# The junction of output projection and MLP: first products begun earlier, odd tiles in PSUM, four squares added later

## The chip, the cores and the metric

One core of one Trainium2 chip runs the kernel; the other cores take no part. The metric is the device time of one execution in microseconds. The program is written with a planner: the kernel's text gives the order of work and its dependencies, the planner lays out each engine's queue from its own costs and then sets the semaphores. Each engine works through its queue in order. Only where the text pins TensorE's instructions do they keep the order of the text.

## The reference, cut to what matters

Two layers; layer 0 mixes with gated DeltaNet, layer 1 with sliding-window attention. Both end in an output projection, and the same gated MLP follows:

```python
for i in range(DEPTH):                       # 2 layers
    hn = rmsnorm(h, norm_mix[i])
    mix = deltanet_mixer(hn, ...) if i % 2 == 0 else swa_mixer(hn, ...)   # ... @ w_out
    h = h + mix
    h = h + conv_ffn(rmsnorm(h, norm_ffn[i]), f_w_up[i], f_conv[i], f_w_down[i])
    gate = sigmoid(rmsnorm(h, norm_ple[i]) @ ple_w_gate[i])
    h = h + gate * (p[i] @ ple_w_proj[i])
return rmsnorm(h, norm_final)

def conv_ffn(x, w_up, conv_w, w_down):
    u = causal_dwconv(x @ w_up, conv_w)      # 1024 -> 2 * 2816, three taps
    gate, val = u[..., :D_FF], u[..., D_FF:]
    return (silu(gate) * val) @ w_down
```

Sequence and model width are 1024, all data f32.

## The kernel before, in words

Activations lie transposed: a tile is 128 channels (partitions) by 1024 positions, two halves of 512; `hs(h)` is a half. h has eight tiles, m = 0 to 7. TensorE multiplies f32 by splitting each operand into a high part (a cast to fp32r, on ScalarE) and a low part (the rest, by a subtraction) and adding three products, high x high, high x low, low x high, in one PSUM bank (`mm3`, L152). For weights the subtraction is on POOL (`load_w`, L199; `halves`, L1193), for activations on VectorE or POOL.

The output projection has two parts. Its first takes the first five mixer tiles (`NP1`) and is fed to TensorE between the mixer's own instructions (`first`). Its last part, `finish`, takes the other three: for each m it loads weights of 384 columns (`add`, with `load_w`), makes 2 x 9 products, and adds the two halves to h (the evictions, L848). Then `Mix.add` prepares the MLP's input from that tile. It stores h in DRAM (hf, L903), scales it by the norm's weight (L906, xw), and forms what the MLP's matrix scheme wants from each pair of an even and an odd tile. The MLP's up projection takes a 2 x 2 block product with seven half-size products in place of eight: of the even tile's halves it needs b11 and t1 (L913, L910), of even and odd tile t2, t3, t4 (L919, L922, L923), of the odd tile b21 and b22, each split in high and low part (`pair`, L897 and L898). At the end the tile is squared and added to the norm's sum (L261, L262).

The MLP, `ffn`, runs over 22 steps j of gate and value tile. Its weights come from two raw tiles a step (L1183, three raw buffers), combined by VectorE into s1 (L1211), s2 (L1212, L1219) and s3 (L1214), and cast and subtracted half by half into three buffers (L1192, L1193); `take` keeps four ahead. A step makes the products b11, t2, t3, t1, b21, t4, b22 with VectorE and ScalarE combining them in PSUM and z1, z2; rows of the norm's factor (`rb`) scale them, and the causal conv (`taps`, L309) and the gate follow, one step later (`gated`). In j = 0 the first four products go k by k, and the sum of squares is closed (`nrm.factor`: 16 small products) right behind them. From j = 2 on, steps of the down projection (`step`, L1285 to L1298) run between: each loads 256 raw columns (`draw`, three buffers) and a tile of h, adds two halves and stores it.

PSUM has three banks for `mm`, three for `d`, two for `s` (`pst`). SBUF working tiles are 40 slots, each given out again after its last use.

TensorE's order is pinned in both mixers and in the MLP; `finish` runs with the pin off.

Of the kernel before, what the change touches and what calls it, by code (L numbers as in the profile page):

```python
# [16 lines left out]
P = 128  # L17
# [91 lines left out]
def kernel(  # L109
# [202 lines left out]
    def delta_layer():  # L312
# [513 lines left out]
        E.pinned = False  # L826
        return op.finish(2, 0)

    class OutProj:
# [13 lines left out]

        def add(self, m, xs, k0):
            t = self.h[m]
            ps2 = proj(self.w[m, :, k0 * P:(k0 + len(xs)) * P], xs)
            for h in range(2):
                V.tensor_tensor(t[:, hs(h)], t[:, hs(h)], ps2[h], ADD)  # L848
# [17 lines left out]
        def finish(self, nxt, l):  # L866
            xs = self.parts(NP1, KT)
            mix = Mix(nxt, l)
            for m in range(KT):
                self.add(m, xs, NP1)  # L870
                if m == KT - 1:
                    for a, b in xs:
                        S.put(a, b)
                mix.add(m, self.h[m])
            return mix

    class Mix:
# [5 lines left out]
        def __init__(self, nxt, l):  # L883
# [3 lines left out]
            self.slots = {n: [] for n in self.x}  # L887

# [3 lines left out]
        def pair(self, t, name, names, eng):  # L892

            hi = S.get(name + "h", F32R)
            lo = S.get(name + "l", F32R)
            for h in range(2):
                A.copy(hi[:, hs(h)], t[:, hs(h)])  # L897
                eng.tensor_tensor(lo[:, hs(h)], t[:, hs(h)], hi[:, hs(h)].bitcast(F32), SUB)  # L898
                self.x[names[h]].append((hi[:, hs(h)], lo[:, hs(h)]))
            self.slots[names[-1]] += [hi, lo]  # L900

        def add(self, m, t):
            nc.sync.dma_start(self.hf[m], t[:, 0:T])  # L903
            xw = S.get("xw")
            for h in range(2):
                A.activation(xw[:, hs(h)], t[:, hs(h)], AF.Copy, scale=self.nrm.w[:, m:m + 1])  # L906
            a, b = hs(0), hs(1)
            if m % 2 == 0:
                self.t12 = S.get("t12")
                V.tensor_tensor(self.t12[:, a], xw[:, a], xw[:, b], SUB)  # L910
                bb = S.get("b11", F32R)
                A.copy(bb[:, a], xw[:, a])
                V.tensor_tensor(bb[:, b], xw[:, a], bb[:, a].bitcast(F32), SUB)  # L913
                self.x["b11"].append((bb[:, a], bb[:, b]))
                self.slots["b11"].append(bb)
                self.xw = xw
            else:
                t12, x0 = self.t12, self.xw
                V.tensor_tensor(t12[:, b], xw[:, b], t12[:, a], ADD)  # L919
                self.pair(t12, "t12", ("t1", "t2"), V)  # L920
                t34 = S.get("t34")
                V.tensor_tensor(t34[:, a], x0[:, b], xw[:, b], SUB)  # L922
                V.tensor_tensor(t34[:, b], xw[:, a], t12[:, b], SUB)  # L923
                S.put(t12, x0)
                self.pair(t34, "t34", ("t3", "t4"), G)
                S.put(t34)
                self.pair(xw, "x1", ("b21", "b22"), G)
                S.put(xw)
            self.nrm.square(t)
            S.put(t)  # L930


    def swa_layer(xs, nrm, hd):
# [235 lines left out]
        E.pinned = False  # L1169
        return op.finish(3, 1)  # L1170
# [4 lines left out]
    def ffn(l, mix, nxt):  # L1175
        nrm, hf = mix.nrm, mix.hf
        E.pinned = True
# [98 lines left out]
        def load_step():  # L1276
# [3 lines left out]
            w = wp.tile([P, 2 * P], F32, tag="draw", name="draw", bufs=3)  # L1280
            nc.sync.dma_start(w, f_down[l, m, :, a * P:(a + 2) * P])
            hi = wp.tile([P, 2 * P], F32R, tag="dhi", name="dhi", bufs=2)
            lo = wp.tile([P, 2 * P], F32R, tag="dlo", name="dlo", bufs=2)
            t = S.get("h")
            nc.sync.dma_start(t[:, 0:T], hf[m])  # L1285
            A.copy(hi, w)  # L1286
            G.tensor_tensor(lo, w, hi[:, :].bitcast(F32), SUB)  # L1287
# [15 lines left out]
        def up(j, early, late):  # L1303
# [6 lines left out]
            if j == 0:  # L1310
                w = take(4)
                ps = [pmt(), pdt(), pmt(), pmt()]
                for k in range(KT // 2):
                    for p, v, xn in zip(ps, w, ("b11", "t2", "t3", "t1")):
                        prod(p, v, xn, (k,))
                p1, p6, p7, p5 = ps
# [4 lines left out]
                nrm.factor()  # L1321
            else:
# [7 lines left out]
                V.tensor_tensor(dd, p6, dd, SUB)  # L1330
                for _ in range(early[1]):
# [12 lines left out]
            if j == 0:  # L1344
                prod(p7, *take(), "t4", first=False)
                rb.extend(nrm.banks())
                A.copy(zh(z1, 0), p1)
                V.tensor_tensor(zh(z1, 0), zh(z1, 0), rb[0], MUL)
                V.tensor_tensor(zh(z2, 1), zh(z2, 1), rb[1], MUL)
            else:  # L1350
                A.copy(zh(z1, 0), p1)
                V.tensor_tensor(zh(z1, 0), zh(z1, 0), rb[0], MUL)
                prod(p7, *take(), "t4", first=False)
            done("t4")
            V.tensor_tensor(zh(z2, 0), p7, dd, ADD)
            V.tensor_tensor(zh(z2, 0), zh(z2, 0), rb[0], MUL)
            for _ in range(late[0]):
                step()
            ys[j] = taps(2 * j + 1, z2)
# [3 lines left out]
            V.tensor_tensor(zh(z1, 1), zh(z1, 1), rb[1], MUL)  # L1363
# [3 lines left out]
        def down(j0, xs):  # L1367
# [31 lines left out]
            return fx, nn  # L1399

# [146 lines left out]
    hT, fx, nrm, ps_in = ffn(0, delta_layer(), 4)  # L1547
# [82 lines left out]
```

## Time and profile before

| | us |
|---|---|
| median of 3 runs | 2816.38 (2813.0 to 2822.61) |
| the profiled execution | 2815.47 |
| its span, first to last instruction | 2813.8 |
| TensorE busy | 2669.6 |
| VectorE busy | 1799.4 |
| ScalarE busy | 1108.4 |
| POOL busy | 1177.4 |

The profile names engines PE (TensorE), DVE (VectorE), ACT (ScalarE), POOL and SP (the queue that issues DMAs). A group of instructions stands as line, engine, operation, written tile <- read tiles and shape. An entry such as "[1.88 <-DVE h L1297]" says how long the engine was idle ahead of an instruction, and what ended that. Times run from the span's start. Busy times of neighbours on VectorE and ScalarE overlap by some 0.08 us, so a queue without a gap shows starts closer together than durations.

### The profile page before, as it was taken

Reading aid. Unit: us, or ns where it says so; the run is one execution under the profiler, and the core shown is the slowest. Engines: PE = TensorE matmul, PEld = TensorE weight load, DVE = VectorE, ACT = ScalarE, POOL = GpSimd, SP = SyncE. Lnnn points to the kernel's source line nnn. Section 1 sums busy time; section 2 is a strip of 40 time slices with the busy share of each in tenths; the row PEclk is TensorE's granted clock in tenths of the full one; section 3 lists DMA queues with packets and bytes.
Section 4 is the critical chain, followed back from the end, with each engine's and each line's share of the span. In section 5 each row is a group of like instructions: output and inputs, shape, how many; then the busy total and the mean of one; then the engine's idle time right before and its main releaser. Section 6 shows DMA issues by size and latency. Waiting matters only on the chain. (4 is left out here: it accounts for less than half of the span.)

```text
span 2813.8 us, 35193 instructions
## 1 busy us (share of the span) xinstructions
PE 2669.6 (95%) x12914; PEld 2144.8 (76%) x12914; DVE 1799.4 (64%) x2491; ACT 1108.4 (39%) x2134; POOL 1177.4 (42%) x1038
## 2 busy tenths in 40 slices
PE   9999999999699999999999998998899999999997
PEld 7777877778487887877777776676677888888786
DVE  6555555563877677677764346646677776767755
ACT  5433433342533333333343235644333333333443
POOL 5444343331654444444432322224544444444344
PEclk9999999999899999999999999999899999999998
DMA  4322222122225555555432221212255555564323
GB/s 171 87 70 63 71 56 63 48 93 61 98 97 182 182 176 199 196 183 178 154 107 77 86 57 45 64 57 95 72 169 184 182 184 186 182 205 159 110 90 107
DMA packets 167070, 340.83 MB, mean 121 GB/s; under 512 B 38897, under 2 KB 91505, under 8 KB 166897
## 3 DMA queue, kind: packets, MB, share of 16 engines
q1 hardware_dynamic: 166032, 337.20, 36.4%
q8 instruction: 101, 1.65, 0.2%
q10 hardware_dynamic: 864, 1.38, 0.1%
q14 instruction: 73, 0.59, 0.1%
HBM read 232.56 MB, written 99.68 MB: 118 GB/s over the span
## 5 line engine op out<-in xcount | busy, mean ns | idle before, releaser
L199 POOL TENSOR_TENSOR wlo<-wraw,whi 128x1024 fp32r<-128x1024 f32 (+4 forms) x138 | 260.6, 1891 | 455.3 <-ACT whi L198 421.0
L152 PE MATMUL mm<-xh,whi 128*128 128x512 f32 x856 | 357.7, 418 | 1.1 <-DVE gt L304 1.0
L152 PE MATMUL mm<-xh,wlo 128*128 128x512 f32 x856 | 349.7, 409 | 0.9 <-POOL wlo L199 0.8
L152 PE MATMUL mm<-xl,whi 128*128 128x512 f32 x856 | 346.4, 405 | 2.5 <-DVE xl L243 2.5
L1287 POOL TENSOR_TENSOR dlo<-draw,dhi 128x256 fp32r<-128x256 f32 x144 | 142.6, 990 | 309.1 <-ACT dhi L1286 287.4
L1193 POOL TENSOR_TENSOR wlo<-sa,whi 128x512 fp32r<-128x512 f32 x132 | 197.5, 1497 | 169.7 <-ACT whi L1192 169.6
L1193 POOL TENSOR_TENSOR wlo<-wraw,whi 128x512 fp32r<-128x512 f32 x132 | 194.6, 1481 | 138.8 <-ACT whi L1192 138.8
L152 PE MATMUL d<-gh,dhi 128*128 128x512 f32 x576 | 229.7, 399 | 12.1 <-DVE h L1297 12.1
L152 PE MATMUL d<-gh,dlo 128*128 128x512 f32 x576 | 227.8, 396 | 0.0
L152 PE MATMUL d<-gl,dhi 128*128 128x512 f32 x576 | 227.8, 395 | 0.0
L1297 DVE TENSOR_TENSOR h<-h,d 128x512 f32<-128x512 f32 x288 | 193.8, 682 | 32.2 <-PE d L152 31.4
L198 ACT CAST whi<-wraw 128x1024 fp32r<-128x1024 f32 (+4 forms) x138 | 108.2, 786 | 266.8 <-PE mm L152 110.5
L152 PEld LDWEIGHTS mm<-xh,wlo 128*128 128x128 f32 x856 | 163.2, 191 | 35.6 <-POOL wlo L199 1.7
L152 PEld LDWEIGHTS mm<-xl,whi 128*128 128x128 f32 x856 | 163.8, 191 | 29.3 <-DVE xl L243 3.4
L152 PEld LDWEIGHTS mm<-xh,whi 128*128 128x128 f32 x856 | 163.6, 191 | 27.9 <-issue 2.0
L309 DVE SCALAR_TENSOR_TENSOR yf<-zg,fcv,yf 128x1024 f32<-128x1024 f32 x88 | 134.9, 1533 | 21.4 <-ACT yf L307 19.9
L152 PEld LDWEIGHTS d<-gh,dhi 128*128 128x128 f32 x576 | 108.2, 188 | 44.9 <-DVE h L1297 15.6
L152 PE MATMUL mm<-t34h,whi 128*128 128x512 f32 x352 | 140.4, 399 | 0.0
L152 PE MATMUL mm<-t34l,whi 128*128 128x512 f32 x352 | 140.4, 399 | 0.0
L152 PE MATMUL mm<-t34h,wlo 128*128 128x512 f32 x352 | 140.2, 398 | 0.0
L152 PE MATMUL mm<-x1h,whi 128*128 128x512 f32 x352 | 139.5, 396 | 0.0
L152 PE MATMUL mm<-x1h,wlo 128*128 128x512 f32 x352 | 139.2, 396 | 0.0
(370 smaller groups left out, 6611.7 us busy)
## 6 DMA issues: line engine op xcount, KB each, us to landing
hf<-h SPq DMA_DIRECT2D x160, 512.0 KB, 3.4
h<-hf SPq DMA_DIRECT2D x160, 512.0 KB, 4.2
wraw<-f_up SPq DMA_DIRECT2D x88, 512.0 KB, 3.4
draw<-f_down SPq DMA_DIRECT2D x144, 128.0 KB, 2.3
wraw<-a_in SPq DMA_DIRECT2D x32, 512.0 KB, 3.4
wraw<-g_w SPq DMA_DIRECT2D x24, 512.0 KB, 3.3
row<-rowd SPq DMA_DIRECT2D x16, 512.0 KB, 3.8
wraw<-b_in SPq DMA_DIRECT2D x12, 512.0 KB, 3.6
```

Source lines behind the costliest of these rows:

```text
L152: i = nc.tensor.matmul(*a, **k)
L198: A.copy(hi, raw)
L199: G.tensor_tensor(lo, raw, hi[:, :].bitcast(F32), SUB)
L309: V.scalar_tensor_tensor(dst[:, 0:T], z[:, i:i + T], w[:, i:i + 1], dst[:, 0:T], MUL, ADD)
L1193: G.tensor_tensor(lo, src, hi.bitcast(F32), SUB)
L1287: G.tensor_tensor(lo, w, hi[:, :].bitcast(F32), SUB)
L1297: V.tensor_tensor(t[:, hs(h)], t[:, hs(h)], ps, ADD)
```

## The change

The MLP becomes a generator that `finish` starts: it takes its first four weights ahead of the last part, makes the k = 0 products of b11 and t1 behind tile 5, and the rest of the first four products behind tile 7. The last part's weights get small buffers of their own (`load_small`, two deep, shared with the down steps, whose raw buffers go from three to two). In `Mix.add` the odd tile is scaled into two PSUM banks (`pst`), and the low parts of b21 and b22 go from POOL to VectorE. Tiles 4 to 7 are squared in place, and their adds and the closing of the sum come later in j = 0. The scaling of j = 0's outputs by the norm's factor and its first conv go to j = 1. TensorE stays pinned from the mixer through the MLP.

```diff
+    def load_small(src, n):
+        raw = wp.tile([P, n], F32, tag="draw", name="draw", bufs=2)
+        nc.sync.dma_start(raw, src)
+        hi = wp.tile([P, n], F32R, tag="dhi", name="dhi", bufs=2)
+        lo = wp.tile([P, n], F32R, tag="dlo", name="dlo", bufs=2)
+        A.copy(hi, raw)
+        G.tensor_tensor(lo, raw, hi[:, :].bitcast(F32), SUB)
+        return hi, lo
...
-        def finish(self, nxt, l):
+        def finish(self, nxt, l, nple):
+            mix = Mix(nxt, l)
+            mlp = ffn(l, mix, nple)
+            next(mlp)
             xs = self.parts(NP1, KT)
-            mix = Mix(nxt, l)
+            E.pinned = True
             for m in range(KT):
-                self.add(m, xs, NP1)
+                t = self.h[m]
+                wh, wl = load_small(self.w[m, :, NP1 * P:], (KT - NP1) * P)
+                for h in range(2):
+                    ps = pdt()
+                    mm3(ps, wh, wl, xs, h)
+                    V.tensor_tensor(t[:, hs(h)], t[:, hs(h)], ps, ADD)
...
+                mix.add(m, t)
+                if m == 5:
+                    next(mlp)
+            return mlp
...
+        def part(self, n, src, hi, lo, eng):
+            A.copy(hi, src)
+            eng.tensor_tensor(lo, src, hi.bitcast(F32), SUB)
+            self.x[n].append((hi, lo))
...
             if m % 2 == 0:
+                x0 = S.get("x0")
+                for h in (a, b):
+                    A.activation(x0[:, h], t[:, h], AF.Copy, scale=w)
                 bb = S.get("b11", F32R)
+                self.part("b11", x0[:, a], bb[:, a], bb[:, b], V)
+                t12 = S.get("t12")
+                V.tensor_tensor(t12[:, a], x0[:, a], x0[:, b], SUB)
+                t12s = S.get("t12h", F32R), S.get("t12l", F32R)
+                self.part("t1", t12[:, a], t12s[0][:, a], t12s[1][:, a], V)
...
             else:
+                x0, t12, t12s = self.even
+                x1 = [pst(), pst()]
+                for h in (1, 0):
+                    A.activation(x1[h], t[:, hs(h)], AF.Copy, scale=w)
                 t34 = S.get("t34")
+                t34s = S.get("t34h", F32R), S.get("t34l", F32R)
+                V.tensor_tensor(t34[:, a], x0[:, b], x1[1], SUB)
+                self.part("t3", t34[:, a], t34s[0][:, a], t34s[1][:, a], G)
+                S.put(x0)
+                V.tensor_tensor(t12[:, b], x1[1], t12[:, a], ADD)
+                self.part("t2", t12[:, b], t12s[0][:, b], t12s[1][:, b], V)
+                V.tensor_tensor(t34[:, b], x1[0], t12[:, b], SUB)
+                self.part("t4", t34[:, b], t34s[0][:, b], t34s[1][:, b], G)
+                S.put(t12, t34)
+                x1s = S.get("x1h", F32R), S.get("x1l", F32R)
+                self.part("b21", x1[0], x1s[0][:, a], x1s[1][:, a], V)
+                self.part("b22", x1[1], x1s[0][:, b], x1s[1][:, b], V)
...
-            self.nrm.square(t)
-            S.put(t)
+            if m < KT // 2:
+                self.nrm.square(t)
+                S.put(t)
+            else:
+                A.activation(t[:, 0:T], t[:, 0:T], AF.Square)
+                self.squares.append(t)
+
+        def sum_squares(self):
+            sq = self.nrm.sq
+            for t in self.squares:
+                V.tensor_tensor(sq[:, 0:T], sq[:, 0:T], t[:, 0:T], ADD)
+                S.put(t)
...
-            w = wp.tile([P, 2 * P], F32, tag="draw", name="draw", bufs=3)
...
+            hi, lo = load_small(f_down[l, m, :, a * P:(a + 2) * P], 2 * P)
...
             if j == 0:
-                w = take(4)
-                ps = [pmt(), pdt(), pmt(), pmt()]
-                for k in range(KT // 2):
-                    for p, v, xn in zip(ps, w, ("b11", "t2", "t3", "t1")):
-                        prod(p, v, xn, (k,))
-                p1, p6, p7, p5 = ps
+                p1, p6, p7, p5 = first
                 A.copy(dd, p1)
...
-                nrm.factor()
             else:
...
+                if j == 1:
+                    rb.extend(nrm.banks())
+                    for z in (z2, z1):
+                        for h in range(2):
+                            V.tensor_tensor(zh(z, h), zh(z, h), rb[h], MUL)
+                        if z is z2:
+                            ys[0] = taps(1, z2)
...
             prod(p1, *take(), "b21", first=False)
+            A.copy(zh(z1, 0), p1)
+            if j:
                 V.tensor_tensor(zh(z1, 0), zh(z1, 0), rb[0], MUL)
+            else:
+                mix.sum_squares()
+            prod(p7, *take(), "t4", first=False)
...
             V.tensor_tensor(zh(z1, 1), p5, dd, SUB)
-            V.tensor_tensor(zh(z1, 1), zh(z1, 1), rb[1], MUL)
+            if j:
+                V.tensor_tensor(zh(z1, 1), zh(z1, 1), rb[1], MUL)
+            else:
+                nrm.factor()
...
+        w = take(4)
+        yield
+        first = pmt(), None, pmt(), pmt()
+
+        def begun(ks):
+            for k in ks:
+                prod(first[0], w[0], "b11", (k,))
+                prod(first[3], w[3], "t1", (k,))
+
+        begun((0,))
+        yield
+        begun(range(1, KT // 2))
+        prod(first[2], w[2], "t3")
+        first = first[0], pdt(), first[2], first[3]
+        prod(first[1], w[1], "t2")
```

## Rows read from the trace of the kernel before

**Rows 1.** The page: the span, and TensorE's busy time, share and instructions.
```profile
span 2813.8 us, 35193 instructions
...
PE 2669.6 (95%) x12914; PEld 2144.8 (76%) x12914; DVE 1799.4 (64%) x2491; ACT 1108.4 (39%) x2134; POOL 1177.4 (42%) x1038
```

**Rows 2.** TensorE's waits over the span: who was waited for, total us, times, longest.
```profile
PE d L152 <- ACT whi L1192: 24.2, 2, 12.3
PE mm L152 <- DVE h L848: 18.4, 6, 5.9
PE d L152 <- DVE h L1297: 12.1, 11, 1.9
```

**Rows 3.** Busy time by stretch: the two junctions, each from first eviction to fourth product's end.
```profile
core 0: us, PE busy (x) PEld busy (x) DVE busy (x) ACT busy (x) POOL busy (x), PEclk, DMA share, GB/s
714.03:782.50 68.47, 45.58 (x176) 33.76 (x174) 56.87 (x59) 41.50 (x67) 44.03 (x28) 0.85 0.32 113
1919.29:1997.18 77.89, 51.20 (x186) 39.03 (x184) 58.20 (x59) 41.23 (x67) 42.63 (x28) 0.80 0.29 102
```

**Rows 4.** TensorE's timeline and chain of waits: start, duration, what (sum's products; twelve products).
```profile
782.34 1.84 PE L152 MATMUL s<-ones,sq 128*128 128x1 f32 x16
...
1997.18 1.68 PE s L152 x16
...
2030.63 2.80 PE d L152 x12
```

**Rows 5.** VectorE's timeline: first evictions of both junctions, and tile pair 2 of J2.
```profile
714.03 1.28 DVE L848 TENSOR_TENSOR h<-h,mm 128x512 f32<-128x512 f32 x2 [1.12 <-PE mm L152]
...
1919.29 0.69 DVE L848 TENSOR_TENSOR h<-h,mm 128x512 f32<-128x512 f32 x1 [1.41 <-PE mm L152]
...
1947.35 1.87 DVE L848 TENSOR_TENSOR h<-h,mm 128x512 f32<-128x512 f32 x3
...
1952.93 1.22 DVE L262 TENSOR_TENSOR sq<-sq,sqt 128x1024 f32<-128x1024 f32 x1
1954.07 0.69 DVE L919 TENSOR_TENSOR t<-xw,t 128x512 f32<-128x512 f32 x1
...
1955.27 1.79 DVE L922 TENSOR_TENSOR t<-xw,xw 128x512 f32<-128x512 f32 x1
...
1960.37 2.28 DVE L262 TENSOR_TENSOR sq<-sq,sqt 128x1024 f32<-128x1024 f32 x1
1962.57 1.87 DVE L848 TENSOR_TENSOR h<-h,mm 128x512 f32<-128x512 f32 x3
```

**Rows 6.** POOL's timeline beside those rows: weights at 1946, activations at 1955.
```profile
1946.31 2.95 POOL L199 TENSOR_TENSOR wlo<-wraw,whi 128x384 fp32r<-128x384 f32 x2
1954.95 3.27 POOL L898 TENSOR_TENSOR x1l<-xw,x1h 128x512 fp32r<-128x512 f32 x2 [5.69 <-ACT x1h L897]
```

**Rows 7.** Timelines of SP, VectorE and ScalarE: the first MLP step's weights in J2.
```profile
1936.71 0.33 SPq L1183 DMA_DIRECT2D wraw<-f_up  x1
...
1977.72 0.68 DVE L1211 TENSOR_TENSOR sa<-wraw 128x512 f32<-128x512 f32 x1
...
1980.08 0.61 ACT L1192 CAST whi<-sa 128x512 fp32r<-128x512 f32 x1
```

**Rows 8.** Timelines of VectorE and TensorE behind J2: taps, and a down step's wait.
```profile
2010.67 1.28 DVE L309 SCALAR_TENSOR_TENSOR yf<-zv,fcv,yf 128x1024 f32<-128x1024 f32 x1
...
2059.05 3.52 DVE L309 SCALAR_TENSOR_TENSOR yf<-zg,fcv,yf 128x1024 f32<-128x1024 f32 x2 [1.99 <-ACT yf L307]
...
2063.31 0.47 PE L152 MATMUL d<-gh,dhi 128*128 128x512 f32 x1 [1.88 <-DVE h L1297]
```

**Rows 9.** The down steps' raw weights: casts, a request (timelines), the page's DMA issues.
```profile
2083.82 0.41 ACT L1286 CAST dhi<-draw 128x256 fp32r<-128x256 f32 x1
2095.03 0.41 ACT L1286 CAST dhi<-draw 128x256 fp32r<-128x256 f32 x1 [2.02 <-DMA hf<-h]
2085.76 0.33 SPq L1281 DMA_DIRECT2D draw<-f_down  x1
...
draw<-f_down SPq DMA_DIRECT2D x144, 128.0 KB, 2.3
```

More of the change, by code (lines that the diff above doesn't have):

```diff
@@ L825, in delta_layer @@
         stage2b(HA - 1, st[HA - 1], zs[HA - 1], 1 << 30)
-        E.pinned = False
-        return op.finish(2, 0)
+        return op.finish(2, 0, 4)
     class OutProj:
@@ L842, in parts @@
             return xs
[L844 to L848, printed above, removed]
         def split_first(self):
@@ L887, in __init__ @@
             self.slots = {n: [] for n in self.x}
+            self.squares = []
         def put(self, n):
             S.put(*self.slots[n])
[L892 to L900, printed above, removed]
+        def part(self, n, src, hi, lo, eng):
+            A.copy(hi, src)
+            eng.tensor_tensor(lo, src, hi.bitcast(F32), SUB)
+            self.x[n].append((hi, lo))
@@ L902, in add @@
         def add(self, m, t):
             nc.sync.dma_start(self.hf[m], t[:, 0:T])
[L904 to L906 removed]
             a, b = hs(0), hs(1)
+            w = self.nrm.w[:, m:m + 1]
             if m % 2 == 0:
[L909 to L910 removed]
+                x0 = S.get("x0")
+                for h in (a, b):
+                    A.activation(x0[:, h], t[:, h], AF.Copy, scale=w)
@@ L915, in add @@
                 self.slots["b11"].append(bb)
-                self.xw = xw
-            else:
-                t12, x0 = self.t12, self.xw
-                V.tensor_tensor(t12[:, b], xw[:, b], t12[:, a], ADD)
-                self.pair(t12, "t12", ("t1", "t2"), V)
+                self.slots["t2"] += t12s
+                self.even = x0, t12, t12s
+            else:
+                x0, t12, t12s = self.even
+                x1 = [pst(), pst()]
+                for h in (1, 0):
+                    A.activation(x1[h], t[:, hs(h)], AF.Copy, scale=w)
@@ L921, in add @@
                 t34 = S.get("t34")
[L922 to L928, printed above, removed]
-            self.nrm.square(t)
-            S.put(t)
+                t34s = S.get("t34h", F32R), S.get("t34l", F32R)
+                V.tensor_tensor(t34[:, a], x0[:, b], x1[1], SUB)
@@ new lines, in add @@
+                self.part("b22", x1[1], x1s[0][:, b], x1s[1][:, b], V)
+                self.slots["t4"] += t34s
+                self.slots["b22"] += x1s
+            if m < KT // 2:
[9 more added lines that the diff above has]
+                S.put(t)
@@ L1168, in swa_layer @@
         S.put(ets, *vt)
-        E.pinned = False
-        return op.finish(3, 1)
+        return op.finish(3, 1, 5)
     fcv = const("fcv", [P, 2 * 2 * NF * CF], f_conv)
@@ L1176, in ffn @@
         nrm, hf = mix.nrm, mix.hf
-        E.pinned = True
         raws = {}
@@ L1545, in last_ple, with outcome @@
         close(1, factor(sq2, t))
-    hT, fx, nrm, ps_in = ffn(0, delta_layer(), 4)
+    def outcome(steps):
+        while True:
+            try:
+                next(steps)
+            except StopIteration as e:
+                return e.value
+    hT, fx, nrm, ps_in = outcome(delta_layer())
     hd = dr.tile([KT, P, T], F32, tag="hd", name="hd")
```

26 lines of the change are left out of this document (5 added, 21 removed).

## The prediction

> **What bounds the kernel now.** I read the page first. TensorE is busy 95% of the span [rows 1], so the kernel is a TensorE stream and a change is worth what it takes out of TensorE's idle time and its half-clock time. The list of who waited for whom then says where the idle time is: two waits of 12 us each for a cast of MLP weights (whi, L1192), 18.4 us in six waits for the eviction h (L848), and 12.1 us in eleven for the eviction of the down steps (L1297) [rows 2]. The first two kinds lie in the two junctions, from the first eviction of an output projection's last part to the end of the MLP's first four products. I call them J1 (714.03 to 782.34, delta layer) and J2 (1919.29 to 1997.18, attention layer) [rows 3, 4, 5]. In J1 TensorE is idle 68.47 - 45.58 = 22.9 us, in J2 77.89 - 51.20 = 26.7 us, at a granted clock of 0.85 and 0.80 [rows 3].
>
> At full clock twelve products of 512 columns take 2.80 us, 0.233 each [rows 4]. From J2's first eviction 144 - 9 + 48 = 183 products remain: 42.7 us, so that nothing but TensorE would end J2 at 1962.0, 35.2 us earlier. In J1 both halves of tile 0 are ready at about 714.6; 174 products, 40.6 us, end at 755.2, 27.1 us earlier. 62.3 us is the most that both junctions can give back.
>
> What holds them is VectorE, busy 56.87 of 68.47 and 58.20 of 77.89 [rows 3]. The reader should follow one pair of tiles: the evictions of pair 2 start at 1947.35, those of pair 3 at 1962.57, a period of 15.2 us [rows 5] against 36 x 0.233 = 8.4 us of products. Evictions follow one another every (1.87 - 0.69)/2 = 0.60 us, a square's add takes 1.14, but some operations stretch: 1.79 for t34 and 2.28 for the square, while POOL works on x1l beside them [rows 5, 6]. And only when the last square is added does VectorE form s1 at 1977.72, from which ScalarE casts weights at 1980.08, though the raw weights were requested at 1936.71 [rows 7]. That is the 12 us wait.
>
> **The change part by part.** The sums are against the profiled execution (2815.47 us, its span 2813.8 and 1.7 around it); the median of three is 2816.38, 0.9 above.
>
> *Weights first.* Six casts, six subtractions and three adds of 512 columns (the first pair's weights) move ahead of the last part. They need raw buffers and weight buffers that the first part of the projection gives back, and nothing else. On the sync queue three raw loads of 512 KB move ahead of the last part's small loads and of the stores; the third waits there for the first part's last raw buffer, with the small loads behind it. VectorE and ScalarE have room there in J2. In J1 they meet the split of the last mixer outputs, on which TensorE waits: between 0 and 2.6 us (two casts and one stretched subtraction in the way, or a small load that lands late); I take 1. With this the 12 us waits go, and what is late next is the chain of the last tiles.
>
> *The chain.* A pair of tiles now costs VectorE four evictions and seven other operations at 0.60, two squares at 1.14 and four stretchings of 1.1 (1.79 against 0.69): 6.6 + 2.3 + 4.4 = 13.3. The rest of the 15.2, 1.9, it is idle. Afterwards: four evictions, three operations on the even tile, six on the odd one, 13 x 0.60 = 7.8; one square's add in pair 0, two in pair 1, none in pairs 2 and 3. POOL has two subtractions of its own fewer per pair, and of the nine others only four read both inputs from SBUF; the nearest rows are evictions (one input in PSUM), which kept 0.60 apart at 1947.35 beside a working POOL [rows 5, 6]. So I take two stretched operations per pair, 2.2 (bounds 0 and 4.4). Pairs: 11.1, 12.3, 10.0, 10.0 = 43.4, and 1 us idle each (bounds 0 and 1.9): 47.4. ScalarE has the same number of operations as before and waits in place of binding. The lower bound of a junction is TensorE's 42.7 and 41.2, the upper 34.6 + 17.6 + 7.6 = 60 if everything stretches and every gap stays; I stand near the middle because the kinds of operation are the measured ones.
>
> A rule speaks against the tiles in PSUM. In the rows one engine alone reads a bank, as the evictions do [rows 5]. The Trainium skill, "PSUM — Partial Sum Buffer", section "PSUM bank collisions raise a hardware error", says that two engines on the same bank and quadrant, reads included, must be kept apart; by it ScalarE's casts of x1 stand behind VectorE's reads of the same bank, some 1 us a pair. No run here shows it. By the rule the sum loses 4 us per junction, without it none.
>
> The last square need no longer precede anything, and in the end only t3's and t2's k = 3 wait for the last tile: their low parts come before the two of x1, so the four products end about when the chain does. The 24 products b11 and t1 fill TensorE meanwhile. J2: 1919.29 + 47.4, with the last three products 1967, gain 30. J1 the same less 1.2 for two evictions that wait for nothing: 760.2, gain 22. Together 52.
>
> *Weights of the last part* in two small buffers in place of three: the cast of tile m+2 waits for the products of m and has 4.2 us for 0.5 + 1.0 to 1.5 plus its queues. On ScalarE the next tile's scaling stands behind a late cast, on POOL the t34 subtraction. Where VectorE sets a pace of 10 to 12 us per pair against 8.4, that costs nothing; if that cover is gone, up to 1 us for each of six tiles. The pinned order of TensorE lets nothing run past it.
>
> *Deferred squares.* Four adds come between the first four products and the sum's 16 small products, 4.6 us alone, 9 if all stretch, with 8.4 us of products (b21, t4, b22) as cover, in which VectorE also has about 4 us of its own. The small products are pinned ahead of j = 1: everything on TensorE stands behind them. 0 to 3.5 us each; I take 1.5. ScalarE's square in place must wait until the store of that tile has read it; nothing else does.
>
> *Scaling deferred* from the MLP's step j = 0 to j = 1: four multiplications (2.4 us) and the two taps of a conv (2.4, by the 1.28 of a tap, 1.2 from start to start [rows 8]) come on VectorE in j = 1. Its load there is then 17 operations of 0.60, six taps of 1.2 and two of 1.14, 19.7, with three stretched some 23, beside 84 x 0.233 = 19.6 us of products. VectorE is late even now: in j = 3 TensorE waits 1.88 us for a down step's eviction that stands behind two taps [rows 8]. From j = 3 on a step has 132 products, 30.8 us, and absorbs it. Bounds 0 and 8 us per layer; I take 3.
>
> *The ring of raw down weights*, 3 to 2, touches all 144 down steps. A request goes out when the low part two steps earlier is made: at 2085.76 for the cast at 2083.82, landing in 2.3, so ready by 2088.1; the step that needs it casts at 2095.03 [rows 9]. Nearly 7 us of cover: nothing. Without the cover every step waits.
>
> Sum: 52 - 1 - 2 x 1.5 - 2 x 3 = 42. 2816.4 - 42 = 2774 us.
>
> **Rivals.**
> (a) TensorE bound. If no operation stretches and the planner fills every gap, the junctions give 62 and the later costs are hidden: 2754. For it: 13 x 0.60 = 7.8 is under 8.4. Against it: pairs 0 and 1 still add squares, 10.1 us in tile pair 1 before any stretching.
> (b) The work is only put off. VectorE's backlog (squares, scaling, taps) costs both upper bounds, 3.5 + 8 per layer, and the chain keeps a pace near 13 per pair (52 in place of 47.4): 52 - 9 - 1 - 23 = 19 gained, 2797. For it: VectorE already starts the first down steps late [rows 8]. Against it: it is idle 19.7 us of J2 [rows 3].
> (c) The weights don't come early: the planner leaves their casts behind the tiles' chain as now, because the last of three weight buffers is free only when the first part's last tile is done. Then 12 us stay in each junction: 42 - 24 = 18 gained, 2798. Against it: only one of three buffers is late, and its weights are needed fifth and sixth. With (b) as well nothing is left: 2816.
> (d) Slower. The ring of two makes the raw down weights land late: the sync queue is in order, and a request held behind a tile's store or load for more than 7 us leaves the step bare. It decides at a loss of 0.35 us a step, 144 x 0.35 = 50, over the 42 gained and the 8.4 that can be told; at 0.5 a step 72 us are lost: 2846. For it: the request does stand behind other waits in that queue. Against it: the 7 us.
>
> **How the numbers follow.** Forecast 0.58, with a range of its own from 2760 to 2790; (a) 0.10; (b) 0.14; (c) 0.06; (b) with (c) 0.05; (d) 0.07. A change under 0.3% (8.4 us) can't be told from none here. Faster: 0.58 + 0.10 + 0.14 + 0.06 = 0.88; same 0.05; slower 0.07. The range runs from (a), 2754, to 2800, just past (b) and (c); (b) with (c), (d) and the tails are left out, less than 0.2.
>
> **What would show it.** Right: the two waits of 12 us for whi gone from TensorE's list; s1, s2, s3 formed before the last part's first eviction; about 10 us between the evictions of pairs 2 and 3, with t34 at 0.69; J2 near 48 us, J1 near 46; waits for L1297 grown by a few us up to j = 3. Wrong: a new wait of TensorE for sq or for the small weights beyond 3 us a junction, a pair period still near 15, idle time before the down steps all through the MLP (d), or a gain that comes from anywhere else than the junctions.

## The result, and the profile after

The changed kernel took 2780.02 us (median of 4, 2775.09 to 2781.53) beside 2814.69 us of the kernel before on the same chip: 34.7 us less, a ratio of 0.9869, 95% interval 0.9845 to 0.9893. Forecast were 2774 and 42 us; the time lies in the range and in the likeliest case's own range.

The page after, beside [rows 1]: the span, and TensorE's, VectorE's, ScalarE's and POOL's busy time.

```profile
span 2779.8 us, 35124 instructions
...
PE 2659.2 (96%) x12914; PEld 2135.3 (77%) x12914; DVE 1790.4 (64%) x2507; ACT 1107.4 (40%) x2134; POOL 1146.3 (41%) x1022
```

TensorE is busy 10.4 us less than in the first trace of the kernel before, but only 2.6 less than in a second one (2661.8): most of the gain is idle time. TensorE's waits after, beside [rows 2] (total, times, longest):

```profile
PE s L152 <- DVE st L786: 12.9, 9, 3.2
PE d L152 <- DVE h L882: 11.2, 4, 4.7
PE d L152 <- DVE h L1321: 10.5, 9, 1.8
...
PE mm L152 <- DVE zv L1361: 4.7, 2, 2.4
```

L786 is the update of the recurrence's state in layer 0 (L776 before, with 8.8 us in all; more under layer 0's tail). L882 is the eviction of the last part (L848 before), L1321 that of the down steps (L1297 before). The two whi waits of 24.2 us are off the list. New are two waits for L1361, the combination of products in j = 1. The two junctions, each from its first eviction to the end of the first four products, beside [rows 3]:

```profile
1908.11:1960.70 52.59, 45.32 (x184) 35.20 (x183) 48.28 (x61) 38.88 (x64) 23.88 (x18) 0.97 0.42 146
723.26:776.00 52.74, 46.58 (x186) 36.20 (x185) 47.19 (x60) 39.05 (x64) 23.76 (x17) 0.94 0.29 106
```

J2 stands first. Counted to the start of the product that follows, J2 is 52.4 us and J1 51.9; the window shown for J1 runs 0.8 us past that point.

TensorE's idle time in J2 went from 26.7 us to 52.59 - 45.32 = 7.3, in J1 from 22.9 to 6.2, and the granted clock from 0.80 and 0.85 to 0.97 and 0.94. VectorE is busy 48.28 of 52.59 us, so it is still the fullest engine there.

Most of the 7.3 us is one wait. VectorE's timeline after, in J2 around tile 4, and TensorE's:

```profile
1926.95 1.21 DVE L272 TENSOR_TENSOR sq<-sq,sqt 128x1024 f32<-128x1024 f32 x1
1928.09 0.68 DVE L910 TENSOR_TENSOR t12l<-t,t12h 128x512 fp32r<-128x512 f32 x1
1928.69 0.67 DVE L937 TENSOR_TENSOR t<-x,s 128x512 f32<-128x512 f32 x1
1929.29 0.68 DVE L940 TENSOR_TENSOR t<-s,t 128x512 f32<-128x512 f32 x1
1929.89 2.04 DVE L272 TENSOR_TENSOR sq<-sq,sqt 128x1024 f32<-128x1024 f32 x1
1931.85 1.74 DVE L910 TENSOR_TENSOR t12l<-t,t12h 128x512 fp32r<-128x512 f32 x1
1933.52 0.68 DVE L942 TENSOR_TENSOR t<-s,t 128x512 f32<-128x512 f32 x1
1934.12 0.67 DVE L910 TENSOR_TENSOR x1l<-s,x1h 128x512 fp32r<-128x512 f32 x1
1934.71 0.67 DVE L882 TENSOR_TENSOR h<-h,d 128x512 f32<-128x512 f32 x1
...
1947.70 1.22 DVE L960 TENSOR_TENSOR sq<-sq,h 128x1024 f32<-128x1024 f32 x1
...
1958.71 2.00 DVE L960 TENSOR_TENSOR sq<-sq,h 128x1024 f32<-128x1024 f32 x1
```

```profile
1935.44 0.50 PE L152 MATMUL d<-oh,dhi 128*128 128x512 f32 x1 [4.71 <-DVE h L882]
```

Follow the lines down: two square adds and a stretched low part of tile pair 1 stand ahead of the eviction at 1934.71, and TensorE idles 4.71 us for the bank it frees. J1 has the same wait of 4.37. The "later" adds (L960) were moved by the planner back into the chain, four from 1947.70 to 1958.71.

### The profile page after: what moved, and what is told of

Same layout as the page of the kernel before. It is cut to its first block, busy times and chain, and to the rows that moved or that the text cites. A ratio compares the mean times of both kernels' runs of the same rounds, so it can differ in the third digit from the quotient of the medians.

```text
span 2779.8 us, 35124 instructions
## 1 busy us (share of the span) xinstructions
PE 2659.2 (96%) x12914; PEld 2135.3 (77%) x12914; DVE 1790.4 (64%) x2507; ACT 1107.4 (40%) x2134; POOL 1146.3 (41%) x1022
## 5 line engine op out<-in xcount | busy, mean ns | idle before, releaser
L199 POOL TENSOR_TENSOR wlo<-wraw,whi 128x1024 fp32r<-128x1024 f32 (+3 forms) x122 | 242.5, 1991 | 397.5 <-ACT whi L198 352.8
L209 POOL TENSOR_TENSOR dlo<-draw,dhi 128x256 fp32r<-128x256 f32 (+1 forms) x160 | 166.2, 1039 | 351.6 <-ACT dhi L208 326.8
L1222 POOL TENSOR_TENSOR wlo<-wraw,whi 128x512 fp32r<-128x512 f32 x132 | 188.4, 1435 | 159.8 <-ACT whi L1221 156.8
L152 PE MATMUL d<-gh,dhi 128*128 128x512 f32 x576 | 229.6, 399 | 10.6 <-DVE h L1321 10.5
L1321 DVE TENSOR_TENSOR h<-h,d 128x512 f32<-128x512 f32 x288 | 193.7, 681 | 32.0 <-PE d L152 31.3
L198 ACT CAST whi<-wraw 128x1024 fp32r<-128x1024 f32 (+3 forms) x122 | 100.0, 822 | 238.8 <-PE mm L152 96.0
L152 PE MATMUL mm<-x1l,whi 128*128 128x512 f32 x352 | 139.4, 396 | 0.2
```

What stands on the lines that cost most here:

```text
L152: i = nc.tensor.matmul(*a, **k)
L1222: G.tensor_tensor(lo, src, hi.bitcast(F32), SUB)
L1321: V.tensor_tensor(t[:, hs(h)], t[:, hs(h)], ps, ADD)
```

## The experiments

The kernels were measured in three groups, each beside the kernel before: the first four rows beside 2811.59 us, the next four beside 2809.14, the last three beside 2811.22. Between groups only the ratios compare. J1 and J2 are read from one trace of each kernel as above (before: J1 68.3 in both of two traces, J2 77.9 and 76.9):

| kernel | us | ratio, 95% interval | J1, J2 us |
|---|---|---|---|
| changed, again | 2776.73 | 0.9878, 0.9863 to 0.9892 | 50.9, 53.4 |
| weights late in the text | 2780.16 | 0.9888, 0.987 to 0.9905 | 54.2, 52.3 |
| odd tile in SBUF | 2794.43 | 0.9944, 0.993 to 0.9957 | 61.6, 60.9 |
| all squares at once | 2791.34 | 0.9929, 0.9911 to 0.9947 | 57.9, 57.8 |
| scaling earlier in j = 1 | 2778.29 | 0.9874, 0.9855 to 0.9893 | 50.9, 52.2 |
| shared buffers | 2782.52 | 0.9896, 0.9878 to 0.9914 | 56.2, 57.1 |
| weights alone | 2797.47 | 0.9951, 0.9932 to 0.997 | 58.7, 58.4 |
| adds later | 2775.59 | 0.9878, 0.9857 to 0.99 | 53.1, 51.3 |
| adds on GpSimd | 2774.68 | 0.9876, 0.9855 to 0.9897 | 51.4, 50.4 |
| the same, scaling earlier | 2770.85 | 0.9861, 0.984 to 0.9882 | 48.3, 52.0 |
| adds on GpSimd, shared buffers | 2786.39 | 0.992, 0.99 to 0.994 | 60.6, 61.2 |

**The changed kernel again.** 

> The changed kernel once more, beside the others on the same chip. Theory A (the junctions carry the gain, the rest of the time moves by chance): ratio to the kernel before 0.987, and the delta layer's last projection part starts within 2 us of where the kernel before has it or of where the first trace of the change has it (714.0 or 723.3), not the same in both executions of the change. Rival B (the change itself costs 9 us in the delta layer): it starts at 723 again.

34.9 us under the kernel before, as theory A's ratio had it. For the start neither theory held: J1 begins at 718.6, between the 714.0 and 723.3 of the first two traces, so a start of J1 read from one trace each says little.

**Weights late in the text.**

```diff
-        w = take(4)
         yield
+        w = take(4)
```

> Undoes one part: the first four weights are taken behind tile 5 in place of ahead of the last part. Theory A (the early weights remove the two waits of 12 us): the casts for tile weights stand behind the tiles' chain again, some 8 to 12 us come back in each junction, 2796 to 2804 us. Rival C (the planner puts ready work into gaps wherever the text has it, and the shorter chain gave the gain): 2778 to 2784, no wait of TensorE for whi over 2 us. If the early weights slow the delta layer's recurrence, that layer's last part starts about 3 us earlier than in the changed kernel.

The rival held: 3.4 us more, within the intervals, and no wait for whi on TensorE's list. The planner formed the weights before the last part's first eviction all the same. Where the request stands in the text decides little.

**Odd tile in SBUF.**

```diff
-                x1 = [pst(), pst()]
+                xs1 = S.get("x1")
+                x1 = [xs1[:, a], xs1[:, b]]
...
+                S.put(xs1)
```

> Undoes one part: the scaled odd tile lies in an SBUF slot in place of two PSUM banks, all engines as in the change. Theory A (one input in PSUM keeps VectorE out of POOL's way): t34 and the low parts of x1 stretch from 0.68 to 1.2 to 1.8 us where POOL works, about 3 us per tile pair on VectorE, junctions longer by 4 to 8 us each, 2788 to 2796. Rival D (TensorE has slack in the tail, or the PSUM banks cost waits of their own): 2776 to 2784.

Theory A held, with junctions that grew by more than it had said: 17.7 us more, both 8 to 10 us longer. Not all of it is the stretching: TensorE now waits 11.3 us for the small weights of the last part (dhi 5.7, dlo 5.6), which the changed kernel does not, and 6.2 in place of 11.2 for the evictions. VectorE's timeline shows the evictions in bursts 14 to 15 us apart, as before the change [rows 5]:

```profile
1930.06 1.87 DVE L882 TENSOR_TENSOR h<-h,d 128x512 f32<-128x512 f32 x3
...
1938.89 1.75 DVE L943 TENSOR_TENSOR t<-x,t 128x512 f32<-128x512 f32 x1
...
1943.99 1.27 DVE L882 TENSOR_TENSOR h<-h,d 128x512 f32<-128x512 f32 x2
```

**All squares at once.**

```diff
-            if m < KT // 2:
+            if m < KT:
```

> Undoes one part: tiles 4 to 7 are squared and added like tiles 0 to 3, at once. Theory A (two adds per pair put the next tile's evictions late, as in pair 1, where TensorE waits 4.4 and 4.7 us): a wait of 3 to 5 us for an eviction in pairs 2 and 3 too, 2786 to 2796. Rival E (the planner already runs the deferred adds inside the chain, at 1947.7 to 1960.7 in the trace, so that deferring them changes nothing): 2777 to 2784.

14.6 us more, 5 to 7 us in each junction. That is theory A's time, but not its sign: no wait for an eviction appears in pairs 2 and 3. In J2 two adds, 3.2 us, stand close ahead of tile 7's evictions (one of 1.22 in the changed kernel), and the last of these starts 45.8 us behind the first eviction (43.0 in the changed kernel). TensorE then waits 1.19 and 1.76 us for the parts of t34 behind the last tile, and its granted clock in J2 is 0.91 in place of 0.97.

**Scaling earlier in j = 1.** The block that makes the banks, scales z2 and z1 and runs the tap is moved ahead of this:

```diff
                 for _ in range(early[0]):
                     step()
                 p6 = pdt()
                 prod(p6, *take(), "t2")
                 V.tensor_tensor(dd, p6, dd, SUB)
-                if j == 1:
-                    rb.extend(nrm.banks())
...
```

> The changed kernel, but in the second down step of each layer the two normalization banks are written, scaled and added into the output tiles ahead of the step's second product in the text, not behind it; the computation is the same. Theory A (TensorE waits in that step 2.35 us for the VectorE scaling of L1361, which stands behind four multiplications and four tap operations): the two waits of 2.3 to 2.4 us go and the time falls by 4 to 5 us, to about 2773 beside the changed kernel's 2776.7 to 2780. Rival (VectorE is the bound of that step, or the inverse root from GpSimd comes last): the wait moves to another line and the time stays within 2 us of the changed kernel's.

The rival held: no measurable gain. The waits for L1361 fall from 4.7 to 1.2 us, but in the 110 us behind J2 those for L1321 rise from 2.7 to 4.4. TensorE's waits there, first of the changed kernel, then of this one:

```profile
PE d L152 <- DVE h L1321: 2.7, 2, 1.8
PE mm L152 <- DVE zv L1361: 2.4, 1, 2.4
```

```profile
PE d L152 <- DVE h L1321: 4.4, 2, 2.6
```

**Shared buffers.**

```diff
-                wh, wl = load_small(self.w[m, :, NP1 * P:], (KT - NP1) * P)
+                wh, wl = load_w(self.w[m, :, NP1 * P:], (KT - NP1) * P)
...
+        yield
+        yield
         w = take(4)
-        yield
...
-        begun((0,))
-        yield
-        begun(range(1, KT // 2))
+        begun(range(KT // 2))
```

> The changed kernel, but the output projection's last part loads its weights into the three buffers that it shared with the MLP's before, and the first pair's weights and products are requested behind all eight tiles; the computation is the same. Theory A (the separate buffers, not the place in the text, let the planner bring the first MLP pair's weights early; taking them away brings back the waits for whi at L1221, 12 us in each layer before): about 12 us of TensorE waits per layer return, the time rises by 16 to 24 us, to 2794 to 2802. Rival (the planner brings the weights early all the same, out of three buffers, as it did where only the place in the text was put back): within 4 us of the changed kernel, at most 2784.

Neither held: 2782.52 is the rival's time, but the weights did come late, as theory A had it. By the ratios the kernel is 5 to 8 us over the changed one, with intervals that overlap. Only the long wait did not come back. VectorE's and TensorE's timelines of this kernel in J2:

```profile
1933.30 1.61 DVE L1240 TENSOR_TENSOR sa<-wraw 128x512 f32<-128x512 f32 x1
...
1951.53 2.33 DVE L960 TENSOR_TENSOR sq<-sq,h 128x1024 f32<-128x1024 f32 x1
```

```profile
1951.12 0.50 PE L152 MATMUL mm<-t34h,whi 128*128 128x512 f32 x1 [2.85 <-ACT whi L1221]
```

s1 is formed inside the last part, 31 us behind the first eviction; before, it stood behind the last square, 58 us behind it [rows 5, 7]. So the 12 us wait for whi falls to 2.85 without the early request. But this kernel keeps another part of the change: b11 and t1 are made for all k ahead of t3 and t2. Before, t2's first product stood second, and TensorE waited there for s2; now the 24 products of b11 and t1, 5.6 us, and the 12 of t3 come ahead of it. The pin of TensorE's order in the last part stays as well. No run undoes either.

**Weights alone.** The odd tile in SBUF and all squares at once, as in the two diffs above, and:

```diff
-                self.part("b21", x1[0], x1s[0][:, a], x1s[1][:, a], V)
-                self.part("b22", x1[1], x1s[0][:, b], x1s[1][:, b], V)
+                self.part("b21", x1[0], x1s[0][:, a], x1s[1][:, a], G)
+                self.part("b22", x1[1], x1s[0][:, b], x1s[1][:, b], G)
```

> The changed kernel with the odd tile of each pair back in SBUF (its low parts on GpSimd, as before the change) and all eight squares added at once: what stays of the change is the early weights with their own buffers, the early first products and the deferred scaling; the computation is the same. Theory A (by the prediction's sum the weights are worth the 12 us wait of each layer, whatever VectorE does): about 2790, 24 us under the kernel before. Rival (the two VectorE edits, 18 and 15 us when undone one at a time, add up, and the early weights without them only move the wait to the evictions): 2806 to 2812, within 6 us of the kernel before.

11.7 us under the kernel before: between the two. What stays is more than the weights: the early and reordered first products are in it, and the deferred scaling with its waits of 4.7 us. No wait for whi, but now TensorE waits for the small buffers, which the VectorE pace of before had been thought to cover:

```profile
1930.29 0.50 PE L152 MATMUL d<-oh,dhi 128*128 128x512 f32 x1 [3.22 <-DVE h L882]
1943.05 0.79 PE L152 MATMUL d<-oh,dhi 128*128 128x512 f32 x1 [4.65 <-ACT dhi L208]
```

**Adds later.** Tiles 1 to 3 are squared into a slot of their own and kept:

```diff
-            if m < KT // 2:
+            if m == 0:
                 self.nrm.square(t)
                 S.put(t)
+            elif m < KT // 2:
+                tmp = S.get("sqt")
+                A.activation(tmp[:, 0:T], t[:, 0:T], AF.Square)
+                S.put(t)
+                self.squares.append(tmp)
...
+            if m == 5:
+                self.sum_squares()
...
+            self.squares = []
```

> The changed kernel, but only the first tile's square is added at once; those of tiles 1 to 5 are added behind tile 5 and those of 6 and 7 in the first down step; the computation is the same. Theory A (the stall of 4.4 to 4.7 us at the eviction of tiles 4 and 5 in each layer comes from the square adds of pair 1 that stand ahead of it on VectorE): the stall shrinks below 2 us in each layer, the time falls by 4 to 9 us, to 2768 to 2775. Rival (the planner puts the adds where VectorE is free to it whatever their place in the text, so the stall stays or moves by a tile): within 2 us of the changed kernel.

The rival held; the wait moves by two tiles and grows. VectorE, then TensorE, in J2:

```profile
1940.41 1.21 DVE L967 TENSOR_TENSOR sq<-sq,h 128x1024 f32<-128x1024 f32 x1
...
1942.14 1.68 DVE L967 TENSOR_TENSOR sq<-sq,h 128x1024 f32<-128x1024 f32 x1
1943.75 1.87 DVE L882 TENSOR_TENSOR h<-h,d 128x512 f32<-128x512 f32 x3
```

```profile
1944.48 0.80 PE L152 MATMUL d<-oh,dhi 128*128 128x512 f32 x1 [6.69 <-DVE h L882]
```

**The kernel before, again.** 

> The kernel before, once more, for a second trace. Theory A (in the changed kernel the early weights of the first MLP step run in the tail of layer 0 and cost that layer 4 to 9 us; its traces and those of its variants with early weights start the last part at 716.0 to 723.5, the kernel before at 714.0 and the one with shared buffers at 714.9): the first eviction of layer 0's last part stands at 713 to 716 again. Rival (the layer's end differs that much from run to run in any kernel): it stands anywhere up to 723.

J1 begins at 715.1: theory A in kind. The four traces without early weights begin it at 714.0 to 715.9, the ten with them at 716.0 to 723.5. But starts scatter from early in the layer on (its first state update, L786, stands at 168.0 to 173.8), and measured over a stretch, below, the weights cost 2.8 us of it.

**Adds on GpSimd**, those of tiles 1 to 3 (by `square(t, G)`) and of 4 to 7:

```diff
-                V.tensor_tensor(sq[:, 0:T], sq[:, 0:T], t[:, 0:T], ADD)
+                G.tensor_tensor(sq[:, 0:T], sq[:, 0:T], t[:, 0:T], ADD)
```

> The changed kernel, but the seven adds of squares of the last part's tiles run on GpSimd (busy 23.9 of 52.6 us there), not on VectorE (48.3 of 52.6); the computation is the same. Theory A (VectorE's queue sets the pace of the evictions, so its total work in the stretch counts, not the order): seven adds at 1.2 to 2.0 us, some 10 us, leave VectorE's queue in each layer, the stretch from the first eviction to the last of the first four products falls from 51 to 53 us to 44 to 47, and the time by 8 to 14 us, to 2764 to 2770. Rival (an add of 1024 columns on GpSimd is long, by the 1.0 to 1.5 us of its 512-column subtractions 2.5 to 3 us or more, and holds up the low parts of t3 and t4 behind it or stretches VectorE's operations): within 4 us of the changed kernel, or above it.

The ratio is that of the changed kernel's repeat (0.9876 and 0.9878): the rival held. The waits for L882 are gone from the list, yet J2 has as much idle time (50.40 - 44.04 = 6.4):

```profile
1906.40:1956.80 50.40, 44.04 (x183) 33.50 (x182) 43.88 (x54) 37.89 (x63) 39.60 (x24) 1.00 0.43 152
```

```profile
1923.42 0.50 PE L152 MATMUL d<-oh,dlo 128*128 128x512 f32 x1 [1.85 <-POOL dlo L209]
1934.41 0.49 PE L152 MATMUL d<-oh,dlo 128*128 128x512 f32 x1 [0.80 <-POOL dlo L209]
1946.94 0.50 PE L152 MATMUL mm<-b,whi 128*128 128x512 f32 x1 [1.23 <-DVE b L910]
1953.46 0.50 PE L152 MATMUL mm<-t34l,whi 128*128 128x512 f32 x1 [2.25 <-POOL t34l L910]
```

An add takes 2.4 to 2.9 us there, POOL is busy 39.60 us in place of 23.88, and TensorE now waits for POOL's low parts.

**The same with the scaling earlier** (both diffs). 

> The changed kernel with the adds of squares on GpSimd and, in the second down step of each layer, the normalization banks scaled and added ahead of the step's second product in the text; the computation is the same. Theory A (the scaling's wait of 2.4 us per layer comes back as a gain once VectorE has room there): 3 to 5 us under the kernel with the adds on GpSimd alone. Rival (moved alone, the scaling gained nothing, since the wait moved on to the evictions of L1321): within 2 us of it.

2770.85 us, the lowest median of all, 3.8 us under the adds on GpSimd alone: theory A's size. But 0.9861 (0.984 to 0.9882) overlaps with the intervals of that kernel and of the changed kernel's repeat (0.9863 to 0.9892): that it is faster than either isn't shown.

**Adds on GpSimd with shared buffers** (both diffs). 

> The changed kernel with the adds of squares on GpSimd, but with the output projection's last part loading into the shared buffers and the first pair's weights and products requested behind all eight tiles, as before the change; the computation is the same. Theory A (early weights are worth more when VectorE is not the bound): 10 us or more over the kernel with the adds on GpSimd and the early weights. Rival (they are worth what they were worth beside the longer VectorE chain, 4 us, since what they save behind the last part they partly cost in the tail of layer 0): 2 to 6 us over it.

11.7 us more than with early weights: theory A in size, but not by its reason. TensorE waits for weights that POOL's adds hold up. In J2 the low part that ends the wait of 4.01 us stands on POOL behind an add of 2.81 and two subtractions, and the cast that ends the wait of 5.32 needs s3, which stands on VectorE behind a low part stretched to 2.24 beside another add.

```profile
PE mm L152 <- ACT whi L1221: 9.4, 2, 5.3
PE mm L152 <- POOL wlo L1222: 8.0, 2, 4.0
```

## Why the prediction was right, and where not

**The sum closes from three places, in part by luck.** Before, J1 and J2 took 68.3 + 77.4 = 145.7 us (means of two traces); after, 51.9 + 52.4 = 104.3 in the first trace, and 104.3 again in the repeat. From these 41.4 go 2.8 in layer 0's tail and 4.7 of waits for L1361: 33.9, beside 34.7 measured. For the repeat the same sum gives 33.9 beside 34.9. Forecast were 52 - 10 = 42: the junctions gave 10.6 less than 52, and the later costs took 2.5 less than 10. With each kernel's own waits for L1361, it gives for the odd tile in SBUF 15.3 (by the ratio 15.7), for all squares at once 22.5 (20.0), for shared buffers, which have nothing in layer 0's tail, 27.5 (29.2). Only the weights alone miss it: 145.7 - 117.1 - 7.5 = 21.1 beside 13.8 by the ratio, with an interval of some 5 to either side; where the rest went stays open. Whole spans are looser than this sum. In the means of two traces each, J1 starts 6.4 us later after the change, of which only 2.8 have a place, and the stretch between J1 and J2 differs by 9.0 us between the two traces of the kernel before alone.

**The chain: the mechanism right, the size off.** This is the term that was mis-sized: 47.4 us from the first eviction to the end of the chain, measured 52. VectorE's idle time was as forecast (4 us; in J2 52.59 - 48.28 = 4.3) and so was the stretching (8.8; the excess over 0.68 and 1.21 us adds up to 7.9). What was short is its work: 43.4 us forecast, 48.3 measured. The four deferred adds, 5.6 us, which the forecast had put behind the products, ran inside the chain.

But less work alone would not have given 47. With the adds on GpSimd VectorE is busy 43.9 us in J2, as forecast, and J2 still takes 50.4: in place of the stall came 6.1 us of smaller waits for VectorE and POOL. The forecast summed VectorE's work over the stretch and had no wait of TensorE for a single late operation in it. Its pairs were 12.1, 13.3, 11.0 and 11.0 us; in J2 the first evictions of the even tiles stand at 1908.1, 1917.8, 1934.7 and 1942.9, which makes 9.7, 16.9, 8.2, and 17.6 to the end of the products. So pair 1 shows a sign that the prediction had named for being wrong, a period near 15: its two square adds fell ahead of pair 2's eviction. Put later, the adds made a wait of 6.69 elsewhere. Pair 3 holds the four adds that the planner moved up, but TensorE had other products there and waited 1.1 us. The durations were right (t34 at 0.67).

**Weights first: right that the wait goes, wrong in why.** The prediction credited the early request with the end of the 12 us waits. Without any of it TensorE waits 2.85 us, and the time rises by 5 to 8 us by the ratios, not by the 24 that rival (c) set for late weights. What had held the casts before was VectorE's queue: in J2 its last square stood ahead of s1 [rows 7]. In J1 s1 was formed at 759.29, before the last square; there the square held up s2, which the stalled product needs. VectorE's timeline before, in J1, then TensorE's in J2:

```profile
763.37 2.29 DVE L262 TENSOR_TENSOR sq<-sq,sqt 128x1024 f32<-128x1024 f32 x1
765.58 1.74 DVE L1212 TENSOR_TENSOR sa<-sa,wraw 128x512 f32<-128x512 f32 x1
```

```profile
1980.74 0.80 PE L152 MATMUL d<-t12h,whi 128*128 128x512 f32 x1 [11.95 <-ACT whi L1192]
```

The kernel with shared buffers gives 27 to 29 us, the one with the weights alone 12 to 14, all together 35: they overlap, and what the first keeps is the larger part. That is the shorter chain together with the new order of the first products and the pin; how much of it the chain gives by itself isn't shown.

**Layer 0's tail: 2.8 us, forecast 1 (0 to 2.6).** The last ten updates of the recurrence's state (L786, first to last) take 69.4 to 69.7 us in all ten kernels with early weights and 66.7 to 67.0 in all four without. Most of it is one place, first in the changed kernel, then with shared buffers:

```profile
693.71 0.35 DVE L786 SCALAR_TENSOR_TENSOR st<-st,egl,s 128x128 f32<-128x128 f32 x1 [2.25 <-PE s L152]
...
698.63 0.69 DVE L1248 TENSOR_TENSOR sa<-sa,wraw 128x512 f32<-128x512 f32 x1 [2.37 <-POOL wlo L1222]
699.24 0.34 DVE L786 SCALAR_TENSOR_TENSOR st<-st,egl,s 128x128 f32<-128x128 f32 x1
```

```profile
687.51 0.35 DVE L786 SCALAR_TENSOR_TENSOR st<-st,egl,s 128x128 f32<-128x128 f32 x1 [2.24 <-PE s L152]
...
691.26 0.35 DVE L786 SCALAR_TENSOR_TENSOR st<-st,egl,s 128x128 f32<-128x128 f32 x1 [1.20 <-PE s L152]
```

The early add of the next weights waits for POOL at the head of VectorE's queue, and the state's update stands behind it: 5.53 us from update to update in place of 3.75, 1.8 of the 2.8. The forecast had named casts and a subtraction there, not an add that itself waits; it counted three adds, and this is a fourth, of the seventh weight. This is part of why late weights cost so little: they save 2.8 us here.

**Deferred squares: cost 0 behind the products, forecast 1.5 each.** The adds ran in the chain, where they are counted above, so the norm's sum found them done; TensorE has no wait for sq. Undone, the edit costs 15 us, since two adds then stand ahead of tile 7's evictions in place of one.

**Scaling deferred: 2.35 us a layer, forecast 3 (0 to 8).** The place was right: four multiplications and four taps ahead of L1361.

```profile
1989.50 0.50 PE L152 MATMUL mm<-t34h,whi 128*128 128x512 f32 x1 [2.35 <-DVE zv L1361]
```

```profile
1984.31 2.32 DVE L319 SCALAR_TENSOR_TENSOR yf<-zv,fcv,yf 128x1024 f32<-128x1024 f32 x1
1986.55 2.29 DVE L319 SCALAR_TENSOR_TENSOR yf<-zg,fcv,yf 128x1024 f32<-128x1024 f32 x1
1988.77 0.68 DVE L1361 TENSOR_TENSOR zv<-mm,sb 128x512 f32<-128x512 f32 x1
```

That the down steps' waits would grow was wrong: 12.1 and 7.1 us for L1297 in two traces before, 10.5 and 6.9 for L1321 after.

**The ring of two: 0, as forecast.** No wait for draw's casts stands on TensorE's list; rival (d) is out. The small buffers cost nothing in the changed kernel, but TensorE waits 9.7 us for their casts in the kernel with weights alone and 11.3 for casts and low parts with the odd tile in SBUF. VectorE's pace is slower in both, and that was the cover that the prediction had named; it did not cover them.

**The tiles in PSUM** are worth 18 us, and the rule weighed against them was not tried. ScalarE's and VectorE's reads of x1 do run at once, unstretched, but on two banks, as far as the order shows. In the last pair of J2 the second low part of x1 (1962.34) releases a product of b21, so the planner took b22 first; by that order the cast below reads b21's bank, the low part b22's:

```profile
1944.74 0.58 ACT L909 CAST x1h<-s 128x512 fp32r<-128x512 f32 x1
```

```profile
1944.70 0.68 DVE L910 TENSOR_TENSOR x1l<-s,x1h 128x512 fp32r<-128x512 f32 x1
```

The Trainium skill ("PSUM — Partial Sum Buffer", "PSUM bank collisions raise a hardware error") asks for distance on the same bank only. By that order no row of the changed kernel's junctions has two engines reading one bank at once, and nothing of the 4 us that the rule was priced at shows in a wait of TensorE.

Of the rivals, (a) failed at the wait of tile 4. (b)'s pace, 52 for the chain, came true, but not its backlog of 11.5 us a layer. (c)'s premise failed in the change, and its price failed where it was made true.

## What to carry to other kernels

When a wait names a late cast, look for what stands ahead of the cast's inputs in the in-order queue, and at which product first needs it: with shared buffers the 12 us wait fell to 2.85 without the earlier request that was meant to remove it. Under a planner the place of an edit in the text was worth little (3.4 us, inside the noise); where the data lie and how many buffers there are was worth more (18 us for the tiles in PSUM, 11.7 for the early weights and their buffers beside the adds on GpSimd). Less work on the fullest engine shortens a stretch only as long as no other engine takes its place: the adds moved to GpSimd gained nothing that can be told. An operation pulled early brings its own waits into a queue where something else is on the path, so each of its inputs must be checked there, not only its duration.

## What the runs showed of the hardware

That it is two inputs from SBUF which make a VectorE operation stretch beside POOL had been an inference from evictions; the kernel with adds on GpSimd shows it side by side. VectorE's timeline there, then POOL's:

```profile
1923.84 0.67 DVE L882 TENSOR_TENSOR h<-h,d 128x512 f32<-128x512 f32 x1
1924.44 2.29 DVE L910 TENSOR_TENSOR t12l<-t,t12h 128x512 fp32r<-128x512 f32 x1
```

```profile
1923.33 2.86 POOL L272 TENSOR_TENSOR sq<-sq,sqt 128x1024 f32<-128x1024 f32 x1
```

The eviction at 1923.84, one input in PSUM, runs beside the add at 0.67; the low part at 1924.44, both inputs in SBUF, lasts until 0.54 us after the add's end at 1926.19. The Trainium skill ("SBUF — State Buffer", "SBUF: two separate sides") says that such an operation of VectorE and one of GpSimd exclude each other for a whole instruction, and these rows agree. So do the junctions of four kernels (before, changed, odd tile in SBUF, adds on GpSimd): the 141 half-tile operations of VectorE that had an input in PSUM and ran beside a POOL instruction took 0.67 to 0.69 us each, the 121 with both inputs in SBUF 0.68 to 2.39. (The prediction set the square at 1960.37 beside POOL's x1l; POOL was then at t34's low parts, with the same effect.) So work moved to GpSimd is paid for twice here: VectorE was rid of seven adds of J2 that had taken 10.6 us, and its busy time there fell by 48.28 - 43.88 = 4.4.

Waits of TensorE have a second price in its clock. Behind the wait of 11.95 us for whi in J2 before, shown above, a product took 0.80 us, at the lower of the two levels (1.2 GHz), and J2's granted clock was 0.80 [rows 3]; after the change it is 0.97, nearly the upper level (2.4 GHz). So part of the gain is not idle time: in J2 TensorE is busy 51.20 - 45.32 = 5.9 us less. Shorter waits can pay it too: behind the 4.71 us shown above a product took 0.50, behind the 4.37 us in J1 0.79, and behind the same 4.71 us in the repeat's J2 0.80.
